# A running log-sum-exp: the carry matmuls of the last chunk moved two chunks ahead, next to those of the tail columns

## The chip, the cores and the metric

One core of one Trainium2 chip. The metric is device time in microseconds of one execution. Where a ratio of two kernels is given, it is the mean time of one kernel's runs over the mean of the other's runs of the same rounds, so it is not quite the ratio of the medians quoted beside it.

## The reference

The input x is float32 of shape (4, 4096, 4128). Along the second axis each row becomes the log-sum-exp of all rows up to it:

```python
out[:, 0, :] = x[:, 0, :]
for t in range(1, S):
    mx = np.maximum(out[:, t - 1, :], x[:, t, :])
    out[:, t, :] = mx + np.log(np.exp(out[:, t - 1, :] - mx) + np.exp(x[:, t, :] - mx))
```

## The kernel before

The kernel computes exp, prefix sums, and log. ScalarE does the exp and the log (Ln), VectorE the additions of rows, and PE, the matrix engine, sums over partitions by matmuls whose results stand in PSUM, in units called banks. DMA brings each tile in from memory and takes it back. A tile is 3 rows (2 in one tile per batch) on each of 128 partitions, all 4128 columns; there are 44 tiles, four of them first in their batch. Four column chunks of 1024 go through it in the order 3, 0, 1, 2; the last 32 columns, "the tail", are done beside chunk 0. Each chunk has two PSUM banks, and the tail, which has none of its own, borrows the first 32 columns of chunk 2's banks.

On PE a chunk's banks collect the rows of the partitions above (`excl`, the "head"), then the own rows (`ident`), then, after the logs are taken, the rest (`below`), so that they hold the running total for the next tile. Chunk 2 can't keep its total there, since the tail uses the bank in between. VectorE copies the total to SBUF (`carry`, in `keep`), and a matmul with the selection matrix `pick` in full fp32 brings it back. All other large matmuls are reduced-precision fp32 (`FP32R`).

```python
order = [NC - 1] + list(range(NC - 1))          # 3, 0, 1, 2
firstc, lastc = order[0], order[-1]
above = [psum.tile([P, CH], FP32, name=f"above{c}") for c in range(NC)]
above_t = above[lastc][:, :tail]
...
    def banks(self, w, cr=None, start=False):
        for s in range(0, CH, MM):
            o = above[self.c][:, s:s + MM]
            if cr is not None:
                mm(o, pick, cr[:, s:s + MM], start=True)
            mm(o, w, self.tot[:, s:s + MM], start=start)

    def head(self):
        through = self.c == lastc and not self.t.first
        self.banks(excl, carry if through else None, start=self.t.first)
...
for g in range(-2, N + 1):            # one chunk a step, over all tiles
    if 0 <= g - 1:
        k = chunks[g - 1]
        k.ln()                        # ScalarE: two Ln
        ...                           # the tail's Ln
        k.complete()                  # PE: below
        if k.c == lastc:
            k.t.store()
            ...                       # load of a later tile
    if g + 2 < N:
        chunks[g + 2].exp()           # ScalarE
    if 0 <= g + 1 < N:
        chunks[g + 1].own()           # VectorE
    if 0 <= g - 1:
        chunks[g - 1].keep()          # VectorE: carry copy, chunk 2 only
    if 0 <= g < N:
        chunks[g].add_above()         # VectorE reads the banks
        chunks[g].add_own()           # PE: ident
        if chunks[g].c == order[1]:
            tail_sums(chunks[g].t)    # PE and VectorE
    if 0 <= g + 1 < N:
        chunks[g + 1].total()         # VectorE: tot
        chunks[g + 1].head()          # PE: excl
```

In the traces each engine runs its own instructions in this order.

The softmax here doesn't subtract the row's maximum and nothing guards it: scores larger than these inputs give would overflow.

Of the kernel before, what the change touches and what calls it, by code (L numbers as in the profile page):

```python
# [13 lines left out]
MM = 512  # L14


def _constants(nc, pool):


    def select(dtype, fill, op, base, step, name):  # L20

        t = pool.tile([P, P], dtype, name=name)
        nc.gpsimd.memset(t.bitcast(FP32), 1.0 - fill)
        nc.gpsimd.affine_select(
            out=t, in_=t, pattern=[[step, P]], compare_op=op, fill=fill, base=base,
            channel_multiplier=-step if step else 1,
        )
        return t

    ge, ne = mybir.AluOpType.is_ge, mybir.AluOpType.not_equal  # L30
    return (
        select(FP32R, 0.0, ge, -1, 1, "excl"),
        select(FP32R, 0.0, ge, -1, -1, "below"),
        select(FP32R, 1.0, ne, 0, 1, "ident"),
        select(FP32, 1.0, ne, 1 - P, 0, "pick"),
    )
# [3 lines left out]
def kernel(  # L40
# [21 lines left out]
    firstc, lastc = order[0], order[-1]  # L62
# [3 lines left out]
    excl, below, ident, pick = _constants(nc, consts)  # L66
# [8 lines left out]
    above = [psum.tile([P, CH], FP32, name=f"above{c}") for c in range(NC)]  # L75
    above_t = above[lastc][:, :tail]
    carry = cpool.tile([P, CH], FP32, name="carry")
# [6 lines left out]
    def mm(o, w, rhs, start=False):  # L84
        nc.tensor.matmul(o, lhsT=w, rhs=rhs, start=start, stop=True, skip_group_check=True)  # L85

    def add(o, a, b):
        nc.vector.tensor_tensor(out=o, in0=a, in1=b, op=mybir.AluOpType.add)  # L88
# [21 lines left out]
    class Chunk:  # L110
# [21 lines left out]
                self.t.tot_t = upool.tile([P, tail], FP32R, name="tot_t")  # L132
                add(self.t.tot_t, x[:, r - 2, t0:], x[:, r - 1, t0:])

        def banks(self, w, cr=None, start=False):
            for s in range(0, CH, MM):
                o = above[self.c][:, s:s + MM]
                if cr is not None:
                    mm(o, pick, cr[:, s:s + MM], start=True)
                mm(o, w, self.tot[:, s:s + MM], start=start)  # L140

        def head(self):

            through = self.c == lastc and not self.t.first
            self.banks(excl, carry if through else None, start=self.t.first)

        def add_above(self):

# [2 lines left out]
            add(v, v, above[self.c].unsqueeze(1).to_broadcast(v.shape))  # L151

        def add_own(self):
            self.banks(ident)

        def keep(self):
            if self.c == lastc and not self.t.final:
# [8 lines left out]
        def complete(self):  # L166

            if self.c != lastc and not self.t.final:
                self.banks(below)

    def tail_sums(t):
        n = t.r - 1
        if not t.first:
            mm(above_t, pick, carry_t, start=True)
        mm(above_t, excl, t.tot_t, start=t.first)
        v = t.xt[:, :n, t0:]
        add(v, v, above_t.unsqueeze(1).to_broadcast(v.shape))
        add(t.xt[:, n, t0:], t.tot_t, above_t)
        if not t.final:
            nc.vector.tensor_copy(carry_t[96:, :], t.xt[96:, n, t0:])  # L180
# [19 lines left out]
    chunks = [Chunk(s, c) for s in steps for c in order]  # L200
    N = len(chunks)
    for g in range(-2, N + 1):
        if 0 <= g - 1:
            k = chunks[g - 1]
            k.ln()
            if k.c == order[1]:
                v = k.t.xt[:, :, t0:]
                nc.scalar.activation(v, v, ACT.Ln)  # L208
            k.complete()
            if k.c == lastc:  # L210
                k.t.store()
                if bufs <= stored + ahead < len(steps):
                    steps[stored + ahead].load()
                stored += 1
        if g + 2 < N:
            chunks[g + 2].exp()
        if 0 <= g + 1 < N:
            chunks[g + 1].own()
        if 0 <= g - 1:
            chunks[g - 1].keep()  # L220
        if 0 <= g < N:
            chunks[g].add_above()
            chunks[g].add_own()
            if chunks[g].c == order[1]:
                tail_sums(chunks[g].t)
        if 0 <= g + 1 < N:
            chunks[g + 1].total()
            chunks[g + 1].head()
# [30 lines left out]
```

## Time and profile before

| | before |
|---|---|
| median of three runs | 1268.28 us |
| profiled execution | 1266.13 us, span 1264.4 us |
| bytes moved | 541 MB, 428 GB/s over the span |
| busiest engine after the DMA | ScalarE, 74% |

The prediction shows the lines on which its argument rests, each with how it is read. The TensorE clock changes during a run (its mean was 0.50 of full speed from 1206 to 1220 us and 0.74 from 1228 to 1236). Below, "cold" is the lower clock, at which a head (two one-pass matmuls) took about 1.24 us from start to release, and "raised" the higher one. In the chain, the number after `x` counts records, and a full-fp32 matmul of 512 columns leaves two records while a reduced-precision one leaves one.

### The profile page before, as it was taken

How to read it: one execution, taken by the hardware profiler on the slowest of the kernel's cores; microseconds unless marked ns; L12 is line 12 of the kernel's file. 1: busy time of each engine (PE TensorE's matmuls, PEld its weight loads, DVE VectorE, ACT ScalarE, POOL GpSimd, SP SyncE). 2: the span in 40 equal slices, each digit the busy share in tenths (PEclk: the TensorE clock that was granted, in tenths of full speed). 3: DMA queues.
4: the chain of work that ended last, by engine and by line, in shares of the span. 5: the costliest groups of instructions: out<-in, count | busy, mean ns of one | idle time of the engine just before them, and what ended most of it. 6: DMA issues, size and time to landing. Idle time of an engine off the chain costs nothing.

```text
span 1264.4 us, 4467 instructions
## 1 busy us (share of the span) xinstructions
PE 653.6 (52%) x1228; PEld 331.8 (26%) x1228; DVE 853.3 (67%) x726; ACT 940.5 (74%) x573; POOL 1.9 (0%) x12
## 2 busy tenths in 40 slices
PE   3555554554355555555445555555543655555553
PEld 1323322222122222222212222222221322222221
DVE  3787767776677677766568677666755777666772
ACT  5888777777777776678678776677876876677783
POOL 0000000000000000000000000000000000000000
PEclk9965655555555555555655555555555555555565
DMA  9999999999999999999999999999999999999997
GB/s 410 412 446 427 426 433 435 431 434 436 429 427 445 428 429 436 434 431 433 433 433 440 427 433 434 433 431 435 430 442 435 428 428 439 431 433 435 434 397 312
DMA packets 12696, 541.34 MB, mean 428 GB/s; under 512 B 1408, under 2 KB 1408, under 8 KB 1408
## 3 DMA queue, kind: packets, MB, share of 16 engines
q1 hardware_dynamic: 12672, 541.07, 99.2%
q8 instruction: 9, 0.15, 0.0%
q14 instruction: 15, 0.12, 0.0%
HBM read 270.53 MB, written 270.53 MB: 428 GB/s over the span
## 4 chain that ended last, share of the span: by engine, by line
DMA 75%; ACT 8%; DVE 6%; PE 6%; issue 4%; ACTq 0%; SPq 0%
DMA xt<-in_x_dram 47%; DMA out_dram<-xt 28%; PE above L85 6%; ACT xt L163 5%; DVE xt L88 4%; ACT xt L164 2%; DVE tot L88 2%; DVE carry L158 1%; ACT xt L120 0%; ACTq L254 0%; DVE carry_t L180 0%; SPq L108 0%; SPq L105 0%; ACTq L120 0%; ACTq L163 0%
## 5 line engine op out<-in xcount | busy, mean ns | idle before, releaser
L120 ACT ACTIVATE xt<-xt 128x3072 f32<-128x3072 f32 (+3 forms) x176 | 474.7, 2698 | 240.8 <-DMA xt<-in_x_dram 240.8
L88 DVE TENSOR_TENSOR xt<-xt,above 128x2048 f32<-128x2048 f32 (+2 forms) x220 | 394.8, 1795 | 136.5 <-PE above L85 135.2
L85 PE MATMUL above<-tot,ident 128*128 128x512 f32 x352 | 204.8, 681 | 336.3 <-DVE xt L88 336.0
L163 ACT ACTIVATE xt<-xt 128x2048 f32<-128x2048 f32 (+1 forms) x176 | 321.0, 1824 | 69.6 <-DVE xt L88 69.3
L85 PE MATMUL above<-tot,excl 128*128 128x512 f32 x352 | 263.7, 827 | 113.8 <-DVE tot L88 97.0
L88 DVE TENSOR_TENSOR xt<-xt 128x1024 f32<-128x1024 f32 (+1 forms) x160 | 196.7, 1229 | 177.0 <-ACT xt L120 175.8
L88 DVE TENSOR_TENSOR tot<-xt 128x1024 fp32r<-128x1024 f32 x176 | 214.8, 1221 | 27.3 <-ACT xt L120 13.0
L85 PE MATMUL above<-tot,below 128*128 128x512 f32 x240 | 131.9, 648 | 147.5 <-ACT xt L164 147.4
L85 PEld LDWEIGHTS above<-tot,ident 128*128 128x128 f32 x352 | 87.2, 301 | 447.2 <-DVE xt L88 444.9
L164 ACT ACTIVATE xt<-above 128x1024 f32<-128x1024 f32 x176 | 177.5, 1008 | 0.9 <-PE above L85 0.9
L85 PEld LDWEIGHTS above<-tot,excl 128*128 128x128 f32 x352 | 92.1, 308 | 216.2 <-DVE tot L88 157.1
L85 PE MATMUL above<-carry,pick 128*128 128x512 f32 x160 | 140.6, 978 | 0.0
L85 PEld LDWEIGHTS above<-tot,below 128*128 128x128 f32 x240 | 64.1, 303 | 215.6 <-ACT xt L164 204.1
L158 DVE COPY carry<-above 32x1024 f32<-32x1024 f32 x40 | 49.2, 1230 | 53.8 <-ACT xt L164 53.8
L85 PEld LDWEIGHTS above<-carry,pick 128*128 128x128 f32 x160 | 52.1, 326 | 31.9 <-issue 20.7
L85 PEld LDWEIGHTS above<-carry_t,pick 128*128 128x128 f32 x80 | 26.4, 330 | 7.7
L85 PE MATMUL above<-carry_t,pick 128*128 128x32 f32 x80 | 18.7, 328 | 0.0
L85 PE MATMUL above<-tot_t,excl 128*128 128x32 f32 x44 | 15.9, 361 | 0.0
L85 PEld LDWEIGHTS above<-tot_t,excl 128*128 128x128 f32 x44 | 14.6, 333 | 0.4
L208 ACT ACTIVATE xt<-xt 128x96 f32<-128x96 f32 (+1 forms) x44 | 12.1, 276 | 0.0
L88 DVE TENSOR_TENSOR tot_t<-xt 128x32 fp32r<-128x32 f32 x44 | 8.1, 184 | 0.0
L180 DVE COPY carry_t<-xt 32x32 f32<-32x32 f32 x40 | 7.1, 178 | 1.4
(16 smaller groups left out, 12.6 us busy)
## 6 DMA issues: line engine op xcount, KB each, us to landing
xt<-in_x_dram SPq DMA_DIRECT2D x40, 6192.0 KB, 43.8
out_dram<-xt SPq DMA_DIRECT2D x40, 6192.0 KB, 32.9
xt<-in_x_dram SPq DMA_DIRECT2D x4, 4128.0 KB, 38.9
out_dram<-xt SPq DMA_DIRECT2D x4, 4128.0 KB, 29.9
```

What stands on the lines that cost most here:

```text
L85: nc.tensor.matmul(o, lhsT=w, rhs=rhs, start=start, stop=True, skip_group_check=True)
L88: nc.vector.tensor_tensor(out=o, in0=a, in1=b, op=mybir.AluOpType.add)
L120: nc.scalar.activation(v, v, ACT.Exp)
L158: nc.vector.tensor_copy(carry[96:, :], above[lastc][96:, :])
L163: nc.scalar.activation(v, v, ACT.Ln)
L164: nc.scalar.activation(t.xt[:, n, a:b], above[self.c], ACT.Ln)
L180: nc.vector.tensor_copy(carry_t[96:, :], t.xt[96:, n, t0:])
L208: nc.scalar.activation(v, v, ACT.Ln)
```

## The change

The intent is to take the carry matmuls off the way to chunk 2's head. They depend only on the previous tile, so they can run as soon as the bank is free, which is when the tail is done.

```diff
-        def banks(self, w, cr=None, start=False):
+        def banks(self, w, rhs, start=False):
             for s in range(0, CH, MM):
-                o = above[self.c][:, s:s + MM]
-                if cr is not None:
-                    mm(o, pick, cr[:, s:s + MM], start=True)
-                mm(o, w, self.tot[:, s:s + MM], start=start)
+                mm(above[self.c][:, s:s + MM], w, rhs[:, s:s + MM], start=start)
+
+        def begin(self):
+
+            if self.c == lastc and not self.t.first:
+                self.banks(pick, carry, start=True)
 
         def head(self):
 
-            through = self.c == lastc and not self.t.first
-            self.banks(excl, carry if through else None, start=self.t.first)
+            self.banks(excl, self.tot, start=self.t.first)
@@ (the other calls of banks now pass self.tot)
             if chunks[g].c == order[1]:
                 tail_sums(chunks[g].t)
+                chunks[g + 2].begin()
```

More of the change, by code (lines that the diff above doesn't have):

```diff
@@ L153, in add_own @@
         def add_own(self):
-            self.banks(ident)
+            self.banks(ident, self.tot)
         def keep(self):
@@ L168, in complete @@
             if self.c != lastc and not self.t.final:
-                self.banks(below)
+                self.banks(below, self.tot)
     def tail_sums(t):
```

## The prediction

> **What bounds the kernel now.** I read the page first: the busy line of the DMA engines and its queue, then the chain that ended last.
>
> ```profile
> PE 653.6 (52%) x1228; PEld 331.8 (26%) x1228; DVE 853.3 (67%) x726; ACT 940.5 (74%) x573; POOL 1.9 (0%) x12
> DMA  9999999999999999999999999999999999999997
> q1 hardware_dynamic: 12672, 541.07, 99.2%
> DMA 75%; ACT 8%; DVE 6%; PE 6%; issue 4%; ACTq 0%; SPq 0%
> ```
>
> No compute engine is above 74%, while the 16 DMA engines are at nine tenths or more in every slice but the last, and the chain is three quarters transfer. 541.07 MB over 1264.4 us is 428 GB/s. The change touches no transfer. So the question is where in the span, if anywhere, the DMA engines wait for compute. The table by stretches answers it (start:end, length, then PE, PEld, DVE, ACT, POOL busy, granted clock, DMA share, GB/s):
>
> ```profile
> 60.00:1228.00 1168.00, 613.78 (x1153) 311.78 (x1153) 808.98 (x683) 884.73 (x533) 0.00 (x0) 0.56 1.00 433
> ...
> 1228.00:1236.00 8.00, 3.19 (x7) 1.60 (x8) 5.61 (x6) 6.14 (x5) 0.00 (x0) 0.74 0.59 254
> ...
> 1244.00:1252.00 8.00, 5.87 (x10) 2.46 (x9) 1.97 (x2) 3.30 (x4) 0.00 (x0) 0.69 0.26 111
> ```
>
> From 60 to 1228 us the DMA share is 1.00. Only the last 36 us have holes. There the last two tiles (call them 42, three rows per partition, and 43, two rows) have been loaded, and nothing is left for the DMA but their stores. The first of these goes out at 1231.7, the last at 1252.5, and both follow the compute chain. This is that chain in order of time (start, length, what), from the tail columns of tile 43:
>
> ```profile
> 1237.95 1.69 PE above L85 x5
> 1239.66 0.28 DVE xt L88 x2
> 1239.94 1.15 DVE tot L88
> 1241.09 0.04 issue
> 1241.13 1.24 PE above L85 x2
> 1242.39 1.23 DVE xt L88
> 1243.62 0.04 issue
> 1243.67 5.48 PE above L85 x8
> 1249.17 1.23 DVE xt L88
> ```
>
> The five matmul records are the own sums of chunk 0 and the tail columns. The two are the head of chunk 1. The eight are chunk 1's own sums (2), the carry matmuls (4 records for 2 matmuls) and the head of chunk 2 (2). So the carry does lie on the path here, inside the 5.48 us.
>
> In the steady state it does not. I read the timeline around the landing of tile 42 at 1195.7. ScalarE waits 6.9 us for that load, then runs an exp, a Ln pair, an exp and another Ln pair without a gap (2.85+1.89+1.0+2.76+1.90+1.01 us, less small overlaps) until the store of tile 41 at 1206.66, 11 us after the landing. The carry and head of tile 41's chunk 2 end at about 1197.8; VectorE only takes that chunk up at 1199.77, after the exp of the new tile. PE has two microseconds to spare.
>
> **What the Trainium skill says.** "FP8 and Floating Point Precision", section "TensorE Precision Notes": true FP32 takes four passes through the array. "TensorE: Matmul & The Clock Gate", section "What's actually happening": the clock is halved to 1.2 GHz until about 3.4 us of sustained activity in a free-running window; "Back-to-back issue gap" in the same page gives N/1.2 ns for a pass when cold. That makes 512/1.2 = 0.427 us, an estimate from the page, for a 512-column pass. The trace agrees: the block of 5.48 us is 2 own sums, 2 carry matmuls of 4 passes and 2 head matmuls, 12 passes, 12 x 0.427 = 5.12, plus about 0.36 us of latency; two one-pass matmuls alone take 1.24 = 0.85 + 0.39. The same block in tile 42 takes only 4.32 us, with a granted clock that rises within it. So the carry is 8 passes, 3.41 us cold and half of that warm. "PSUM — Partial Sum Buffer", section "PSUM bank collisions raise a hardware error", says to guard PSUM by bank and not by address; here even addresses overlap, since the tail columns use the first 32 columns of chunk 2's bank, so the carry must wait for both VectorE reads of the tail. The built program has that wait on VectorE at the first carry matmul. "DMA: Bandwidth & Descriptors", section "Specifications", gives 435 GB/s as the fabric's ceiling; the 433 of the long stretch sits on it, so nothing is to be had there by ordering compute.
>
> **The change part by part.** Nothing is removed: the same 2 carry matmuls (160 records for 40 tiles) run per tile that has a predecessor in its batch. They move from between chunk 1's own sums and chunk 2's head to between the tail matmuls and chunk 1's head. The weights also change less often (carry, carry, head, head in place of carry, head, carry, head), which I take as worth nothing. VectorE, ScalarE and the issuing queue keep their order.
>
> Cost at chunk 1, tile 43, clock cold: the carry may start when the second tail add is done, about 1239.95, and takes 3.41, to 1243.36. Chunk 1's sum is ready at 1241.1, so its head, which ran 1241.13 to 1242.37, now runs 1243.36 to 1244.60. That is 2.2 us later. PE was idle 1.5 us there (1239.6 to 1241.1), so of the carry's 3.4 us only about 1.2 is hidden.
>
> Gain at chunk 2: VectorE adds chunk 1 from 1244.62 to 1245.85, makes chunk 2's sum by 1246.97 (1.12 behind the add), and the head of two passes with its latency takes 1.24, to 1248.25. From the end of chunk 1's add to the start of chunk 2's add is thus 2.4 us in place of 5.5: 3.1 gained. Balance of tile 43: chunk 2's add at 1248.27 against 1249.17, **0.9 us gained**. Warm, the carry is 1.7 us, both sides shrink, and the balance is near zero to half a microsecond.
>
> Tile 42, same sums: the tail adds end at 1217.04, carry to 1220.5, head to 1221.7 against 1219.80, so 1.9 later; chunk 1's add to 1224.05, sum at 1225.16, head to 1226.4; chunk 2's add at 1226.45 against 1226.51. **About 0** if all is cold, because the block it replaces was already half warm (4.32). If the clock rises inside the new block instead, up to 1.5 more.
>
> Sum at the end: 0.9 + 0 to 0.5 = about 1.2 us. The last store begins with an empty queue, so its start moves one for one with the end.
>
> The first 140 us: the chain runs through compute there too (5 tiles, blocks of 4.3 to 5.5 us), so the stores are issued perhaps a microsecond per tile sooner. But the DMA share stays near 1.0 there, since a load or another store is always outstanding. Gain 0. The 36 or so tiles of the steady state: 0. There chunk 1's add ends about 26.4 us after a tile's landing and would end at 28.3; the Ln that needs it follows the next tile's exp, which ends at about 29.5 + 2.85 = 32.3. Four microseconds of room.
>
> **Rivals.**
> *The carry was on the path in every tile.* Then 40 tiles x 0.9 to 1.5 would be 36 to 60 us and the time 1208 to 1232. For it: chunk 2's adds do wait for the long block (135.2 us of VectorE idle behind PE in all). Against it: the 1.00 DMA share and 433 GB/s from 60 to 1228; the bytes alone at 433 GB/s need 1250 us. I give it under 1%.
> *The added wait and the later head of chunk 1 become a new bound.* If each of 40 tiles lost 2 us it would be 1348. For it: PE stands still for the tail adds, and chunk 1's head is held back by about 2 us. Against it: the four microseconds of room, and chunk 2 gets it back within the same tile. If only the two last tiles lose (a warm block becomes cold), the time is 1269 to 1270. Some 15% for such a small loss, under 1% for a large one.
> *Earlier stores change how loads and stores interleave.* Slices range from 426 to 446 GB/s in the steady state. An unlucky or lucky mix of 0.2% is 2.5 us either way. This is what widens the range most.
>
> **Range and chances.** Before is 1268.28, three runs within 0.21. Less 1.2 gives 1267.1. The end effect spans -3 to +1.5 and the interleaving about 2 either way, so 1264.6 to 1269.4. 2% is 25.4 us, which needs one of the first two rivals in its large form: faster 0.5%, slower 0.5%, within 99%.
>
> **What would show it.** The DMA share from 60 to 1228 stays 1.00, at 431 to 435 GB/s. The carry's weight loads now wait for VectorE, briefly (about 0.4 us behind the tail matmuls). In the chain of the last two tiles the block of eight splits into two and two, and the head of chunk 1 is released about 2 us later after the tail. ScalarE's wait for loads stays near 240.8 us. VectorE's wait for PE (135.2) falls in front of chunk 2 and rises in front of chunk 1, changing little in sum; that sum says nothing about the time. I am wrong if the DMA share of the long stretch drops below 0.99, if ScalarE's wait for loads shrinks by tens of microseconds while its wait for VectorE grows, or if the last 36 us move by more than 3.

## The result, and the profile after

| | before | after |
|---|---|---|
| median | 1268.29 us (1268.09 to 1268.77, 4 runs) | 1265.59 us (1264.17 to 1266.48, 4 runs) |
| ratio | | 0.9977, 95% interval 0.9960 to 0.9994 |
| span of the profiled run | 1264.4 us | 1262.5 us |

The page's chain and DMA queue of the kernel after:

```profile
q1 hardware_dynamic: 12672, 541.07, 99.3%
DMA 75%; ACT 9%; PE 6%; DVE 5%; issue 4%; SPq 0%; ACTq 0%
```

The table by stretches, of the kernel after. The columns are those of the prediction; the last two are DMA share and GB/s:

```profile
60.00:1228.00 1168.00, 618.76 (x1153) 298.26 (x1152) 808.64 (x683) 883.85 (x533) 0.00 (x0) 0.56 1.00 433
1228.00:1264.00 36.00, 13.47 (x25) 6.10 (x25) 10.97 (x12) 14.72 (x14) 0.00 (x0) 0.55 0.72 309
```

The long stretch is what it was: a DMA share of 1.00 at 433 GB/s. So a gain is to be looked for at the end. This is the chain of tile 43 after the change, from the same point as in the prediction (here and in the chains below, pieces under 0.1 us are left out without a mark):

```profile
1237.22 1.69 PE above L85 x5
1238.93 0.29 DVE xt L88 x2
1239.27 4.29 PE above L85 x6
1243.58 1.22 DVE xt L88
1244.80 1.15 DVE tot L88
1245.99 0.92 PE above L85 x2
1246.94 1.23 DVE xt L88
```

The carry now starts when the two tail adds are done and shares a block with chunk 1's head (4 + 2 records). VectorE takes up chunk 1 at 6.36 us after the first line, where it was 4.44: 1.9 us later. It takes up chunk 2 at 9.72 us, where it was 11.22: 1.5 us earlier. The block of 5.48 is gone; what stands between the two adds is VectorE's own sum and a head of 0.92 us, which here ran at the raised clock.

Tile 42 is another story. The chain of the kernel before, then of the kernel after:

```profile
1222.16 4.32 PE above L85 x8
1226.51 2.30 DVE xt L88
1228.89 1.92 ACT xt L163
```

```profile
1216.59 4.65 PE above L85 x6
1221.26 2.30 DVE xt L88
1223.64 1.91 ACT xt L164
1225.56 0.91 ACT xt L165
1226.47 1.38 ACT xt L120
...
1228.17 1.90 ACT xt L164
```

Before, chunk 2's Ln started when VectorE had added chunk 2. After, it started when ScalarE was through with the Ln of chunk 1 (late, because chunk 1 is late) and the exp of the next tile's chunk 0. In this profile the chain has moved from PE to ScalarE. Counted from the landing of the tile (1195.72 and 1195.21), this Ln came at 33.17 us and now comes at 32.96: 0.2 us gained. Two other profiles with the new order here, told below, do not show the move: in `after_again` and `last_two` the Ln follows VectorE's add of chunk 2, with ScalarE's exp done less than 0.1 us earlier, and the gain was 0.1 and 0.7 us. The head of chunk 2 ran there at the cold clock (1.22 us of PE time, against 0.74 here). So ScalarE's order is a limit close by, and which of the two engines comes last differs between these profiles.

### The profile page after: what moved, and what is told of

It is laid out like the page before. It is cut to its first block, busy times and chain, and to the rows that moved or that the text cites. A ratio compares the mean times of both kernels' runs of the same rounds, so it can differ in the third digit from the quotient of the medians. Undisturbed runs are those within 1.5% of the kernel's fastest.

```text
span 1262.5 us, 4467 instructions
## 1 busy us (share of the span) xinstructions
PE 660.3 (52%) x1228; PEld 318.0 (25%) x1228; DVE 853.3 (68%) x726; ACT 939.9 (74%) x573; POOL 1.9 (0%) x12
## 4 chain that ended last, share of the span: by engine, by line
DMA 75%; ACT 9%; PE 6%; DVE 5%; issue 4%; SPq 0%; ACTq 0%
DMA xt<-in_x_dram 47%; DMA out_dram<-xt 28%; ACT xt L164 6%; PE above L85 6%; DVE xt L88 3%; ACT xt L165 3%; DVE tot L88 1%; ACT xt L120 1%; DVE carry L159 1%; SPq L108 0%; SPq L105 0%; ACTq L120 0%; ACTq L164 0%
## 5 line engine op out<-in xcount | busy, mean ns | idle before, releaser
L120 ACT ACTIVATE xt<-xt 128x3072 f32<-128x3072 f32 (+3 forms) x176 | 474.8, 2699 | 245.5 <-DMA xt<-in_x_dram 245.5
L88 DVE TENSOR_TENSOR xt<-xt,above 128x2048 f32<-128x2048 f32 (+2 forms) x220 | 394.9, 1795 | 180.1 <-PE above L85 178.3
L85 PE MATMUL above<-tot,ident 128*128 128x512 f32 x352 | 192.2, 643 | 334.5 <-DVE xt L88 334.2
L85 PE MATMUL above<-tot,excl 128*128 128x512 f32 x352 | 224.8, 736 | 52.4 <-DVE tot L88 35.5
L85 PEld LDWEIGHTS above<-tot,ident 128*128 128x128 f32 x352 | 82.8, 284 | 439.4 <-DVE xt L88 437.1
L85 PE MATMUL above<-carry,pick 128*128 128x512 f32 x160 | 149.7, 1091 | 16.3 <-DVE xt L88 16.3
L85 PEld LDWEIGHTS above<-carry,pick 128*128 128x128 f32 x160 | 47.0, 324 | 62.0 <-issue 41.3
```

Source lines behind the costliest of these rows:

```text
L85: nc.tensor.matmul(o, lhsT=w, rhs=rhs, start=start, stop=True, skip_group_check=True)
L88: nc.vector.tensor_tensor(out=o, in0=a, in1=b, op=mybir.AluOpType.add)
L120: nc.scalar.activation(v, v, ACT.Exp)
```

## The experiments

Those with the full stores gave correct results. The kernel before ran beside each, with medians of 1267.23, 1267.23 and 1267.20 us on three chips.

**The same kernel again; the change in the last two tiles only; in all others only.** The first is the changed kernel unchanged. In the other two the condition of `begin` and `head` is narrowed, and tiles outside it keep the old order (the lines are shortened: in the runs the first two terms stand in a helper, `through()`, and `head` has the reverse test):

```diff
-            if self.c == lastc and not self.t.first:
+            if self.c == lastc and not self.t.first and self.t in steps[-2:]:       # last_two
+            if self.c == lastc and not self.t.first and self.t not in steps[-2:]:   # all_but_last_two
```

> The changed kernel once more, on the chip of the next three. End-of-chain theory: about 1265.6 us, 2 to 3 us under the kernel before. If the 2.7 us of the first comparison were partly luck, the difference shrinks towards the 1.5 us that the last two tiles' chain shows.

> The carry comes early in the last two tiles only; the other 38 keep the old order. End-of-chain theory: the whole gain, 1.5 to 2.7 us, as in the changed kernel (about 1265.6). Rival, that an earlier or later store in the middle changes how loads and stores mix: no gain, about 1268.3.

> The reverse: early in all tiles but the last two. End-of-chain theory: no gain, 1267.5 to 1269 us, and a DMA share of 1.00 in the long stretch. Rival (mix of loads and stores): the gain of the changed kernel, about 1265.6.

Measured in the same rounds, against 1267.23 us (1266.47 to 1268.50, 9 runs): the changed kernel 1266.46 (ratio 0.9989, 0.9976 to 1.0003), the last two only 1265.88 (0.9986, 0.9973 to 0.9998), all others only 1267.57 (0.9998, 0.9985 to 1.0011). Every run of the last-two kernel (1265.27 to 1266.44) is shorter than every run of the other (1266.75 to 1267.77). The gain is in the last two tiles; 38 tiles with the new order give none that shows. And the changed kernel's gain on this chip is 1.4 us by the means (1266.11 against 1267.48), not 2.7. Its interval reaches 1.0003, so by the clock alone it is barely told from nothing. The profiles are sharper, since they allow to count from the landing of tile 42, the last full tile, and so leave out when the DMA got there. There is one profile for each kernel. The carry copy is VectorE's `keep` after chunk 2 and marks the end of tile 42; the last Ln is taken at its start:

| kernel | tile 42 lands | landing to carry copy | carry copy to last Ln | landing to end of span |
|---|---|---|---|---|
| before | 1195.72 | 36.02 | 19.71 | 68.7 |
| after | 1195.21 | 35.80 | 18.46 | 67.3 |
| after, again | 1196.39 | 35.91 | 18.65 | 67.5 |
| last two only | 1196.83 | 35.29 | 18.65 | 67.0 |
| all but last two | 1196.51 | 36.64 | 19.73 | 69.4 |
| split (below) | 1197.15 | 34.09 | 16.94 | 64.2 |
| after chunk 1's head (below) | 1196.71 | 34.43 | 17.84 | 65.2 |

Where the last two tiles have the new order, tile 43 takes 1.1 to 1.3 us less than in the kernel before and tile 42 0.1 to 0.7 us. The first stands clear: the two kernels with the old order there agree within 0.02 us (19.71 and 19.73). The second does not, since the same two differ by 0.6 us in tile 42 (36.02 and 36.64; the block with the carry took 4.32 us in one and 4.93 in the other). The landing itself lies between 1195.2 and 1197.2 in no order that goes with the change. A scatter of 2 us there is as large as the gain, and can blur the run times.

**The carry split over two idle slots of PE.** Bank 1, which the tail does not use, gets its carry at the tail; bank 0 gets it after chunk 1's head:

```diff
-        def begin(self):
+        def begin(self, s):
             if self.c == lastc and not self.t.first:
-                self.banks(pick, carry, start=True)
+                mm(above[self.c][:, s:s + MM], pick, carry[:, s:s + MM], start=True)
@@
-                chunks[g + 2].begin()
+                chunks[g + 2].begin(MM)
@@
             chunks[g + 1].head()
+            if chunks[g + 1].c == order[2]:
+                chunks[g + 2].begin(0)
```

> The carry of bank 1 stays at the tail columns, that of bank 0 (which the tail uses) comes after chunk 1's head, where PE waits for VectorE. If the delay of chunk 1's head by the carry is what eats part of the gain: head of chunk 1 back at its old time, chunk 2's add about 2 us earlier than before in tile 42 and 3 in tile 43, in sum 1263 to 1264.5 us, 1 to 2.5 us under the changed kernel. If ScalarE and not PE sets the end there: no better than the changed kernel, 1265 to 1266.

1262.72 us (1261.76 to 1263.12, 5 runs), ratio 0.9961 (0.9948 to 0.9973): 4.5 us under the kernel before by the medians, 3.7 under the changed one. The chain of tile 43:

```profile
1239.50 2.94 PE above L85 x4
1242.47 1.22 DVE xt L88
1243.69 1.15 DVE tot L88
1244.88 0.75 PE above L85 x2
1245.65 1.23 DVE xt L88
```

Chunk 1's head is back within 0.6 us of its old time (5.0 us after the tail's block began at 1237.45, where it was 4.44). In the table tile 42 gains 1.9 us and tile 43 2.8, near the expected 2 and 3. So the delay of chunk 1 was indeed what ate most of the gain. This version beats both.

**Few stores: the same three placements with compute as the bound.** To see what a tile gains when the DMA does not hide it, only columns 0 to 1023 were stored:

```diff
-            nc.sync.dma_start(out=self.dram(out), in_=self.xt)
+            nc.sync.dma_start(out=self.dram(out)[:, :, :CH], in_=self.xt[:, :, :CH])
```

> The kernel before with only columns 0 to 1023 of each tile stored (wrong result on purpose): a quarter of the store bytes, so that compute bounds and not the DMA. 338 MB at about 430 GB/s would take 790 us; the compute chain of the first 140 us ran 24.6 to 26.4 us a tile, 25.4 in the mean. With about 43 tiles' worth that is 1060 to 1130 us. Serves as the base of the next two.

> The changed kernel with the same few stores. My step sums (0 to 0.9 us a tile, 1.3 where the clock warms): 0 to 50 us under the other few-stores kernel, most likely 10 to 40. Rival, that the held-back head of chunk 1 costs what chunk 2 gains: within 5 us of it.

> The split placement with the same few stores. If the carry fits into the two idle slots of PE: 2 to 3 us a tile under the kernel before with few stores, 60 to 120 us less, unless ScalarE becomes the bound first: its 940 us of work plus waits for the start give a floor near 960 us.

1114.89, 1107.24 and 1045.81 us. Their outputs are wrong, which doesn't matter for the times. The DMA share from 200 to 1000 us is 0.76 in the first, so the bound is compute. Over the 40 tiles that have a carry, the change is worth 7.65/40 = 0.19 us a tile, the split placement 69.1/40 = 1.73. The result for the change is below the 10 to 40 us that I thought most likely. The chain shows why. With few stores, the kernel before:

```profile
603.08 5.47 PE above L85 x8
608.58 2.30 DVE xt L88
...
610.96 1.91 ACT xt L163
```

and the changed kernel:

```profile
601.84 1.91 ACT xt L164
603.76 0.91 ACT xt L165
604.67 1.87 ACT xt L120
...
607.22 1.90 ACT xt L164
```

The first goes through PE's long block to VectorE and the Ln of chunk 2. The second goes through ScalarE: Ln of the late chunk 1, exp, Ln of chunk 2, as in tile 42 above.

**ScalarE's order.** If that order is the cause, moving the exp into the gap where ScalarE waits for chunk 1 must bring the missing part:

```diff
     for g in range(-2, N + 1):
+        early = 0 <= g < N and chunks[g].c == lastc and g + 2 < N
+        if early:
+            chunks[g + 2].exp()
         if 0 <= g - 1:
             k = chunks[g - 1]
             k.ln()
@@
-        if g + 2 < N:
+        if g + 2 < N and not early:
```

> Few stores, old carry placement, and on ScalarE the exp of the next tile's chunk 0 comes ahead of the Ln of chunk 1, in the gap where it waits (wrong result on purpose, as all few-stores runs). The long PE block holds chunk 2 back well past ScalarE here, so nothing should change: 1112 to 1117 us.

> Few stores, changed carry placement, the same ScalarE order. If ScalarE's fixed order (Ln of the delayed chunk 1, then an exp, then the Ln of chunk 2) is what ate most of the step sum's 0.9 us a tile: about 0.7 us a tile more, 1075 to 1090 us, and chunk 2's Ln waits for VectorE again. Rival, that PE's clock or the wait for the tail adds ate it: still 1105 to 1109.

1122.20 and 1084.31 us. With the changed placement ScalarE's new order takes another 22.9 us, 0.57 a tile. Its chain goes through VectorE again, and chunk 2's Ln waits for VectorE's add:

```profile
615.97 1.22 DVE tot L88
...
618.27 2.29 DVE xt L88
620.64 1.91 ACT xt L164
```

Under that order the change is worth 37.9/40 = 0.95 us a tile, or 30.6/40 = 0.76 if it is set against the faster of the two kernels with the old placement; under the old order it was 0.19. With the old placement I expected no difference and it got 7.3 us slower. That miss stays open. Its chain has the same blocks as without the exp moved, and the loss isn't even over the tiles: of the 9.0 us between the two profiles, 2.0 lie before the first carry copy, 3.1 at the three changes of batch and 1.1 after the last copy, and only 2.8 in the 36 steps in between, nearly all of it in the stretch that holds the block with the carry. Why is not shown.

**The whole carry after chunk 1's head.** `begin()` called where the split version calls `begin(0)`, and not at the tail.

> Full stores. The whole carry after chunk 1's head, none at the tail. Chunk 1 is not delayed; in tile 42 about 2.9 us of the carry lie beside VectorE's add and sum, in tile 43 (add of one row) less. Step sums with a cold clock: chunk 2's add 0.5 to 0.7 us earlier in tile 42 and 1.7 in tile 43, so 1264.5 to 1266 us; the split placement should stay 1.5 to 3 us better.

1263.79 us (1263.66 to 1264.87, 5 runs), ratio 0.9975 (0.9963 to 0.9988), with 1267.20 for the kernel before. That is better than expected: the gains were 1.6 us in tile 42, where the clock rose inside the longer block, and 1.9 in tile 43. Against the split version, by ratios of different chips, it gives away about 0.0014 or 1.8 us, with intervals that overlap; counted from the landing of tile 42 it is 1.0 us (65.2 less 64.2).

**A carry of one pass.** Old order, with `pick` and `carry` as FP32R. One of the edited lines is shown; `pick` is changed likewise, and the tail's own carry matmul reads it as full fp32, as before:

```diff
-    carry = cpool.tile([P, CH], FP32, name="carry")
+    carry = cpool.tile([P, CH], FP32R, name="carry")
```

> The old order, but the carry as reduced-precision fp32: one pass in place of four, 2 records in place of 4, 2.6 us less per cold block (6 passes of 0.427). The result may be less exact, perhaps outside the tolerance; this is to measure the cost. End-of-chain theory: the block of 5.48 becomes about 2.9 but the head waits for VectorE's sum anyway, so 2 to 3 us gained in each of the last two tiles, 1263 to 1265 us. If the passes are not what costs, 1268.

1263.58 us (1263.23 to 1263.97, 4 runs), ratio 0.9973 (0.9959 to 0.9988), and the result was correct within the tolerance. The block that took 5.48 us now takes 2.94: 2.54 us for six passes fewer, 0.42 each. The passes are what costs. Tile 43 took 2.5 us less, as expected, but tile 42 only 1.4, where I had expected 2 to 3: the block it replaced there was already partly at the raised clock (4.32).

**Both together.**

> The split placement with the carry as reduced-precision fp32 (one pass instead of four). In the split the carry of bank 1 still delays chunk 1's head by about 0.5 us (the block was 2.94 from its start, the head alone 1.24); with one pass that delay goes. 0.5 to 1.5 us under the split placement: about 1261 to 1262.5.

1262.21 us (1261.69 to 1263.59, 5 runs), ratio 0.9962 (0.9949 to 0.9974): the same as the split alone. In its profile the landing to end takes 64.2 us, as in the split's. I had expected 0.5 to 1.5 us. The gain at chunk 1 was there: from the end of the tail adds to VectorE's add of chunk 1 the split took 3.01 us in tile 42 and in tile 43, this version 2.77 and 2.44. But PE stayed cold. No pair of one-pass matmuls in its whole trace took under 1.0 us, while in the split's trace some eighty took under 0.8. In tile 43 chunk 2's head took 1.22 us where it took 0.73 in the split, and the 0.57 us gained at chunk 1 was 0.5 lost again. (The page lists a granted clock of 1.00 for this run. These times contradict it, so it isn't used.) That the fewer passes kept PE cold is likely but not shown.

## Why the prediction was right

**The bound.** Right: the DMA share from 60 to 1228 us was 1.00 at 433 GB/s in the kernel before, after, and in every full-store experiment. The rival with the carry on the path in every tile (1208 to 1232 us) is out: the change in 38 tiles alone gave 1267.57 us. ScalarE's wait for loads went from 240.8 to 245.5 us, near what I said.

**The size.** I predicted 1.2 us, all of it at the end. The first comparison gave 2.7 by the medians, the second 1.4 by the means; counted from the landing the profiles say 1.4 and 1.2 (68.7 less 67.3 and 67.5). The rest of the 2.7 is scatter between runs and chips, to which the 2 us in tile 42's landing belong; the runs don't separate its parts. That the first comparison showed more than twice the predicted gain was luck. The range had allowed for such scatter: 1264.6 to 1269.4 held.

**Tile 43.** 0.9 us predicted with a cold clock, at chunk 2's add. Counted from the carry copy that add came 1.3 to 1.5 us earlier in the three runs that had the change, and the last Ln 1.1 to 1.3. The cold block of carry and head measured 4.65 us, against 8 + 2 passes at the prediction's estimate of 0.427 and 0.36 of latency, 4.63. In two of the three it took just that; the head of chunk 2 then took 0.75 at the raised clock, where I had 1.24. That half microsecond is what the estimate missed: it had only all cold, or all warm with a smaller gain, and not a cold carry followed by a head at the raised clock.

**Tile 42.** 0 to 0.5 predicted, 0.1 to 0.7 measured, no clearer than the scatter of this tile (0.6 us between two old orders). The step was also incomplete. I wrote that VectorE and ScalarE keep their order and took this as harmless; kept order is what let the late chunk 1 push back an exp and with it chunk 2's Ln. VectorE was ready 0.49 us earlier in the first profile of the change and the Ln came only 0.2 us earlier. There, with the DMA as bound, this cost 0.3 us; in the two other profiles it cost nothing. With few stores it cost 0.57 to 0.76 us a tile (0.76 or 0.95, less 0.19), three quarters or more of what PE and VectorE had gained.

**The first 140 us.** I wrote that stores would go out about a microsecond per tile sooner, though without effect. They did not: the fourth and fifth went out at 113.85 and 139.55 us against 114.42 and 139.48.

**VectorE's wait for PE.** I said it would change little in sum. It rose from 135.2 to 178.3 us. The two lines that matter, before and then after:

```profile
DVE xt L88 <- ACT xt L120: 175.8, 46, 8.8
DVE xt L88 <- PE above L85: 135.2, 142, 4.4
```

```profile
DVE xt L88 <- PE above L85: 178.3, 136, 3.6
DVE xt L88 <- ACT xt L120: 121.4, 38, 8.8
```

The wait for ScalarE's exp fell by 54 us at the same time. In the steady state VectorE stands and waits for the next load's exp anyway, as I had found for chunk 2; a later chunk 1 only moves some of that waiting under PE's name. As I did say, the sum tells nothing of the time.

## What to carry to other kernels

Here the DMA share was 1.00 through the middle, and the change to compute paid only where the DMA ran dry, in the last 36 us. In such a case find the few tiles that lie there and work the sum out for those. When work is moved ahead on an in-order engine, it delays whatever it is put in front of, so put it where the engine waits and the next thing isn't ready (the split placement gained 4.9 us where the change gained 1.4, by the means of the same rounds), and follow the delayed thing into the other engines' fixed orders. To see what a hidden change is worth, take the bound away: with few stores the same three placements lay 69 us apart.

## What the Trainium skill lacked or had wrong

- "DMA: Bandwidth & Descriptors", section "Where 436 GB/s comes from", says that for transfers between HBM and SBUF the HBM side at about 358 GB/s binds, though the same passage notes a measurement of 425 as near the fabric's rate. The first is too general for a core that runs alone. Here one core moved 433 GB/s, half of it reads and half writes, for 1168 us on end, at the fabric's figure, with no other core used by the program.
- "TensorE: Matmul & The Clock Gate", section "Back-to-back issue gap", gives a gap for N columns without saying that it is for one pass. A full-fp32 matmul took four such passes: the block with a one-pass carry was shorter by 2.54 us for six passes, 0.42 us each at 512 columns.
- No page says how a full-fp32 matmul appears in a trace: two records for one matmul of four passes (160 records for 80 matmuls here).
